# Three ways to feed float32 weights to TensorE in the mixer: split in two parts on ACT and VectorE, split by an accumulating DMA, or not split

## The chip, the cores and the metric

The kernel runs on one core of one Trainium2 chip. The metric is the time of one execution on the device in microseconds (us). One core has TensorE (PE, with its weight loads shown apart as PEld), VectorE (DVE), ScalarE (ACT), GpSimd (POOL) and SyncE (SP), which here issues loads, and 16 DMA engines that all transfers share.

## What is computed

Three layers in float32 on one sequence of 256 tokens with 1024 features. All of the change lies in the mixer of the first one.

```python
def mixer_sublayer(h, w_in, ...):               # h is 256 x 1024
    proj = h @ w_in
    conv_in, z, xbc, dt_raw, g_conv, g_ssm = jnp.split(proj, splits, axis=-1)
    a_half, b_half = jnp.split(conv_in, 2, axis=-1)
    u = a_half * sigmoid(b_half)
    u = causal_depthwise_conv(u, conv_dw_w, conv_dw_b)          # 31 taps
    y_conv = silu(layer_norm(u, ...)) @ w_conv_out
    xbc = silu(causal_depthwise_conv(xbc, ssm_conv_w, ssm_conv_b))
    xs, bm, cm = jnp.split(xbc, ...)
    dt = softplus(dt_raw + dt_bias)
    y = ssd_chunked_scan(xs, dt, -exp(a_log), bm, cm) + d_skip * xs   # 4 groups
    y = rmsnorm_per_group(y * silu(z)) * ssm_norm_w
    y_ssm = y @ w_ssm_out
    return (sigmoid(g_conv) * y_conv + sigmoid(g_ssm) * y_ssm) @ w_out
# block: h = rms_norm(x) * (1 + scale) + shift, where shift, scale = silu(c) @ w_ada + b
```

Behind it come a feed-forward layer, a gated-delta layer with an MLP and a gated-linear-attention layer with an MLP, each with a norm.

## The kernel before

**Items.** A weight matrix is cut into items of 128 x 1024 float32 (512 KB). One call of `w3` (L155) prepares one: SP loads it into a slot of the ring "raw", which has 6 (L150 to L153), and it is split into a rounded part hi and a remainder lo, both in TensorE's reduced float32 format (fp32r), in slots of the ring "w", which has 8, so four items. The slot of raw is free again when the splitting has read it. The activations h are split in the same manner into hh and hl, and `mm3` (L184 to L188) makes each product of three fp32r matmuls: hi by hi (L186), hi by lo (L187 or L188) and lo by hi.

**Two ways to split.** In the way called S here, ACT casts hi (L170) and DVE subtracts it from raw (L171). In the way called D, ACT writes minus raw to lo (L166), a DMA that POOL issues adds raw onto it while rounding (L167), and ACT casts hi (L168); so lo is the rounding remainder, and DVE has no part in it, but 512 KB more go through the DMA engines. A counter `nw` of the calls of `w3` decides: in the state space and the gates, calls after the 14th whose number isn't a multiple of 4 are D (L178), all others are S. By call numbers:
- 1 to 8, w_abe in `start`, S
- 9, w_dt (the step sizes dt), S
- 10 to 19, w_ab (gated input of the long convolution), 20 to 27, w_bc (B and C)
- 28 to 59, four groups g0 to g3, each with four items of w_xs and four of w_z
- 60 to 75, w_g (the gates).

So 34 of the state space's 51 items are D and 17 S; of the gates' 16, 12 are D and 4 S. Items of w_z make four products of 512 columns each (`proj_tok`, L204); all others make eight of 256 columns (`projA` with `mmA`).

**What runs beside it.** The 31 taps of the long convolution are 240 instructions on DVE (L501, from and to acc), spread over the time between w_ab and the merge, where `conv_ln` (L791) reads the result. The next layers' modulation weights (ada) are loaded into the same ring and reduced by DVE (L410). In each group, POOL and ACT build the right-hand sides srhs of the segment sums (L343, L349), PE multiplies (L352), ACT takes the exponential E (L679), DVE masks it (L681) and PE contracts it with xdt (L686). `mix_gates` (L718) leaves the tanh of the gates; `merge` then begins with w_ssm_out (psa<-yT).

**Order.** Each engine runs its own list of instructions in order. The lists are made ahead of time by a scheduler, from the program, its dependencies and the rings; SP's list of loads and POOL's list of accumulating DMAs are among them, so an instruction that waits holds up all behind it on its engine.

Of the kernel before, what the change touches and what calls it, by code (L numbers as in the profile page):

```python
# [18 lines left out]
P = 128  # L19
T = 256  # L20
D = 1024
# [45 lines left out]

NW = 14

# [41 lines left out]
class K:  # L111
    def __init__(self, ctx, tc, A):
        self.tc, self.nc, self.A = tc, tc.nc, A
        pool = lambda name, **kw: ctx.enter_context(tc.tile_pool(name=name, **kw))
        self.cp = pool("cp", bufs=1)
        self.px = pool("px", bufs=1)
        self.dp = pool("dp", bufs=1, space=bass.MemoryType.DRAM)
        self.wp = pool("wp", bufs=1)
        self.wx = self.big = self.sm = self.ps = self.kp = None
        self.n = self.nw = 0  # L120
        self.pending = None
        self.dma_lo = 0

# [31 lines left out]
    def w3(self, name, i, nk, extra=False):  # L155

        nc = self.nc
        if extra and self.wx is not None:
            hi, lo = (self.wx.tile([P, 1024], F32R, tag="wx", name=self.nm(v)) for v in ("xhi", "xlo"))
        else:  # L160
            hi, lo = (self.wp.tile([P, 1024], F32R, tag="w", bufs=8, name=self.nm(v)) for v in ("whi", "wlo"))
        t = self.raw(self.A[name][i])
        hi, lo = (v[:, : t.shape[-1]] for v in (hi, lo))
        self.nw += 1
        if self.dma_lo and self.nw > NW and self.nw % self.dma_lo:
            nc.scalar.activation(out=lo, in_=t, func=AF.Copy, scale=-1.0)  # L166
            nc.gpsimd.dma_start(out=lo, in_=t, accum_op=ALU.add)  # L167
            nc.scalar.copy(hi, t)  # L168
        else:
            nc.scalar.copy(hi, t)  # L170
            nc.vector.tensor_tensor(out=lo, in0=t, in1=hi.bitcast(F32), op=ALU.subtract)  # L171
# [18 lines left out]
    def mmA(self, out, w, x):  # L190


        for k in range(8):
            xh, xl = x(k) if callable(x) else (x[0][:, :, k, :], x[1][:, :, k, :])
            self.mm3(out, w[0][:, k], w[1][:, k], xh, xl, k == 0, k == 7)
# [9 lines left out]
    def proj_tok(self, name, i0, x, evac, early=False):  # L205
# [4 lines left out]
        def one(c, w, t):  # L210
            for k2 in range(2):
                k = 2 * c + k2
                self.mm3(b[t], x[0][:, t, k], x[1][:, t, k], w[0][:, k2], w[1][:, k2], k == 0, k == 7)

# [100 lines left out]

    def xpose_split(self, src, t, hi, lo, scale=None, bias=None, nk=8, ks=None, n=4):

        nc = self.nc
        n = min(nk, n)
        for k0 in ks or range(0, nk, n):  # L320
# [5 lines left out]
            if scale is None:  # L326
                nc.scalar.copy(h, b3)  # L327
                nc.vector.tensor_tensor(out=l, in0=b3, in1=h.bitcast(F32), op=ALU.subtract)  # L328
                continue
            f = self.smt([P, 4, P], "f")[:, :n]  # L330
            for kk in range(n):
# [185 lines left out]
    def start(self):  # L517
# [13 lines left out]
        for k in range(8):  # L531
            self.ada("w_ada_mix", k, mod)
            self.ada("w_ada_mix", 8 + k, mod)
            if k == 0:
                xn = [self.rms_tok(self.x[:, t]) for t in range(2)]
            self.ada_bias(mod, "b_ada_mix", k, k + 1)
            self.ada_bias(mod, "b_ada_mix", k + 8, k + 9)
            self.ada_scale(mod, "norm_mix_w", a, k, 1)
            for t in range(2):
                self.xpose_split(xn[t], t, h[0], h[1], a, mod[:, 0:8], ks=(k,), n=1)  # L540
            wh, wl = self.w3("w_abe", k, 6)
# [456 lines left out]
    def gdn(self, h):  # L998
# [44 lines left out]
        proj_z(0, True)  # L1043
        self.dma_lo = 5
        kT = self.bigt([P, 8, T], name="kT")
# [507 lines left out]
def tile_kernel(ctx, tc, A):  # L1553
    k = K(ctx, tc, A)
    nc = tc.nc
    with ExitStack() as st:
        k.kp = st.enter_context(tc.tile_pool(name="kp", bufs=1))
        with k.phase("mixer", 0, 0, 3, 3, 2):
            with k.phase("ssm", 1, 0, 0, 0, 0):
                k.dma_lo = 4  # L1560
                h, banks = k.start()
                yT, acc = k.state_space(h, banks)
                tg = k.mix_gates(h)
            k.dma_lo = 0
            with k.phase("mix", 0, 8, 0, 0, 0):
                mh = k.merge(yT, acc, tg)
    k.dma_lo = 0
    k.spill = k.dp.tile([P, 2, D], F32, name="spill")
    with k.phase("ffn", 0, 16, 2, 4, 2):
        h = k.feed_forward(mh)  # L1570
    with k.phase("gdn", 8, 0, 2, 3, 3):
        k.more_masks(M_R, M_LEV + 2)
        oT = k.gdn(h)
    k.dma_lo = 0
    with k.phase("mlp0", 0, 16, 2, 4, 2):
# [143 lines left out]
```

## Time and profile before

| | |
|---|---|
| runs of the kernel | 1437.17, 1437.42, 1441.13 us, median 1437.42 |
| the profiled execution's own time | 1445.81 us |
| its span (first to last instruction) | 1444.0 us |
| PE busy in the span | 1313.5 us (91%) |
| DVE, ACT, POOL busy | 994.4 (69%), 753.0 (52%), 160.7 us (11%) |
| loads by SP (hardware queue) | 224.08 MB, 45.0% of the DMA engines' time |
| DMAs by POOL (software queue) | 46.28 MB, 15.5% |

The span is read by stages, which the first matmuls of each kind mark on PE: `start` to 44.3 us, w_dt, w_ab, w_bc and g0's first w_xs items to 131, the groups' middles to 175, 214, 253, the end of g3 with the first gates to 283, the gates to 328.7, where `merge` begins. An engine's busy time against the length of a stage says how much of the stage it could explain; the waits say what ended the rest. PEclk is the granted TensorE clock as a share of the full 2.4 GHz.

### The profile page before, as it was taken

The numbers are of one execution on the slowest core, as the hardware profiler recorded it, in microseconds if no ns is written. First come the engines' busy times: TensorE is split into PE (matmuls) and PEld (weight loads), VectorE is DVE, ScalarE is ACT, GpSimd is POOL, SyncE is SP. The second block draws the span as 40 slices with busy tenths as digits, with TensorE's granted clock in tenths as the row PEclk, the third lists the DMA queues.
The fourth block names the chain that finished last, engine by engine and source line by source line (L and its number), as shares of the span: only waits on it lengthen the run. The fifth ranks groups of instructions, "written<-read, shape, count | busy, mean of one in ns | idle before, by whom it ended". The sixth has DMA issues, their size and how long they took to land. (4 is left out here: it accounts for less than half of the span.)

```text
span 1444.0 us, 21885 instructions
## 1 busy us (share of the span) xinstructions
PE 1313.5 (91%) x8408; PEld 1180.2 (82%) x8408; DVE 994.4 (69%) x1800; ACT 753.0 (52%) x1199; POOL 160.7 (11%) x176
## 2 busy tenths in 40 slices
PE   5899899879998999998768878899999998999997
PEld 4897788869987999977767766789997986788896
DVE  7878899669577665743679974865465796765453
ACT  4666687735446443636686523544353645454440
POOL 0212232210000000012511430000001000000000
PEclk9999999989899999999879989999999999999999
DMA  9899789998265765639458313765364313576430
GB/s 339 285 267 254 200 226 238 280 280 329 89 219 169 261 214 188 209 124 231 114 141 229 88 44 123 255 208 188 131 219 144 118 61 115 177 248 213 154 128 30
DMA packets 74616, 271.76 MB, mean 188 GB/s; under 512 B 8559, under 2 KB 8687, under 8 KB 74000
## 3 DMA queue, kind: packets, MB, share of 16 engines
q1 hardware_dynamic: 62208, 224.08, 45.0%
q0 software_dynamic: 12304, 46.28, 15.5%
q8 instruction: 66, 1.08, 0.3%
q14 instruction: 38, 0.31, 0.1%
HBM read 232.06 MB, written 2.10 MB: 162 GB/s over the span
## 5 line engine op out<-in xcount | busy, mean ns | idle before, releaser
L188 PE MATMUL psa<-hh,wlo 128*128 128x256 f32 x1448 | 419.3, 290 | 27.0 <-DMA wlo<-raw 24.9
L186 PE MATMUL psa<-hh,whi 128*128 128x256 f32 x1448 | 419.1, 290 | 2.3 <-ACT hh L180 1.3
L187 PE MATMUL psa<-hl,whi 128*128 128x256 f32 x1448 | 417.6, 288 | 0.8 <-DVE hl L181 0.5
L171 DVE TENSOR_TENSOR wlo<-raw,whi 128x1024 fp32r<-128x1024 f32 (+1 forms) x206 | 248.0, 1211 | 152.2 <-ACT whi L170 144.0
L170 ACT CAST whi<-raw 128x1024 fp32r<-128x1024 f32 (+1 forms) x206 | 213.4, 1041 | 216.4 <-PE psa L187 149.8
L188 PEld LDWEIGHTS psa<-hh,wlo 128*128 128x128 f32 x1448 | 284.1, 196 | 32.6 <-DMA wlo<-raw 28.5
L186 PEld LDWEIGHTS psa<-hh,whi 128*128 128x128 f32 x1448 | 284.4, 196 | 6.5 <-ACT hh L180 2.9
L187 PEld LDWEIGHTS psa<-hl,whi 128*128 128x128 f32 x1448 | 283.7, 196 | 3.9 <-DVE hl L181 1.8
L171 DVE TENSOR_TENSOR xlo<-raw,xhi 128x1024 fp32r<-128x1024 f32 x100 | 121.1, 1221 | 64.5 <-ACT xhi L170 64.1
L170 ACT CAST xhi<-raw 128x1024 fp32r<-128x1024 f32 x100 | 104.8, 1050 | 95.7 <-DMA raw<-in_w_mlp 60.7
L186 PE MATMUL psb<-xhi,hid 128*128 128x512 f32 x344 | 136.2, 396 | 1.0 <-ACT hid L327 0.9
L188 PE MATMUL psb<-xhi,hidl 128*128 128x512 f32 x344 | 136.2, 396 | 0.0
L187 PE MATMUL psb<-xlo,hid 128*128 128x512 f32 x344 | 135.7, 395 | 0.0
L501 DVE SCALAR_TENSOR_TENSOR acc<-u,vecs,acc 128x229 f32<-128x229 f32 (+28 forms) x240 | 104.8, 479 | 0.3
L166 ACT ACTIVATE wlo<-raw 128x1024 fp32r<-128x1024 f32 x69 | 73.0, 1058 | 49.0 <-PE psa L187 25.5
L187 PE MATMUL psa<-wlo,hh 128*128 128x512 f32 x208 | 83.4, 402 | 5.4 <-DVE wlo L171 3.6
L167 POOL DMA_DIRECT2D wlo<-raw x69 | 60.1, 870 | 247.4 <-ACT wlo L166 200.8
L186 PE MATMUL psa<-whi,hh 128*128 128x512 f32 x208 | 84.1, 406 | 2.1 <-ACT hh L180 1.5
L410 DVE CUSTOM_DVE_ANT_0 raw<-raw,g 128x1024 f32<-128x1024 f32 x48 | 58.6, 1220 | 37.6 <-DMA raw<-in_w_ada_ffn 21.9
L188 PE MATMUL psa<-whi,hl 128*128 128x512 f32 x208 | 82.9, 401 | 0.6 <-DVE hl L181 0.6
L188 PEld LDWEIGHTS psb<-xhi,hidl 128*128 128x128 f32 x344 | 64.7, 188 | 15.3 <-DVE hidl L181 0.3
L186 PEld LDWEIGHTS psb<-xhi,hid 128*128 128x128 f32 x344 | 64.8, 188 | 15.0 <-ACT hid L327 1.4
(388 smaller groups left out, 2230.8 us busy)
## 6 DMA issues: line engine op xcount, KB each, us to landing
raw<-in_w_mlp SPq DMA_DIRECT2D x120, 512.0 KB, 4.1
wlo<-raw POOLq DMA_DIRECT2D x69, 512.0 KB, 7.2
raw<-in_w_ffn_in SPq DMA_DIRECT2D x40, 512.0 KB, 4.2
raw<-in_w_ada_mix SPq DMA_DIRECT2D x24, 512.0 KB, 5.8
raw<-in_w_ada_ffn SPq DMA_DIRECT2D x24, 512.0 KB, 4.5
raw<-in_w_qkv SPq DMA_DIRECT2D x24, 512.0 KB, 5.6
raw<-in_w_ffn_down SPq DMA_DIRECT2D x22, 512.0 KB, 4.2
raw<-in_w_xs SPq DMA_DIRECT2D x16, 512.0 KB, 5.2
```

The lines of the kernel that those rows point to most:

```text
L166: nc.scalar.activation(out=lo, in_=t, func=AF.Copy, scale=-1.0)
L167: nc.gpsimd.dma_start(out=lo, in_=t, accum_op=ALU.add)
L170: nc.scalar.copy(hi, t)
L171: nc.vector.tensor_tensor(out=lo, in0=t, in1=hi.bitcast(F32), op=ALU.subtract)
L186: mm(out, ah, bh, start=start, stop=False)
L187: mm(out, ah, bl, start=False, stop=False)
L188: mm(out, al, bh, start=False, stop=stop)
L410: self.nc.vector.tensor_tensor_reduce(out=w, in0=w, in1=self.sc, scale=1.0, scalar=0.0, op0=ALU.mult, op1=ALU.add, accum_out=mod[:, i : i ...
L501: nc.vector.scalar_tensor_tensor(out=o, in0=i, scalar=taps[:, j : j + 1], in1=o, op0=ALU.mult, op1=ALU.add)
```

## The change

Three forms of an item are named by letters, and a string gives the turn: the form of call number `nw` is `form[nw % len(form)]`. N is new: the raw item itself is the operand of float32 matmuls, one for each product in place of three, with h kept in float32 beside its two halves. Nothing is split for it, and its slot of raw stays taken until PE has read it.

```diff
-NW = 14
+FORM_SSM = "NDNS"
+FORM_GATES = "SD"
+FORM_GDN = "SDDDD"
...
+        self.nw += 1
+        form = self.form[self.nw % len(self.form)]
+        if form == "N":
+            return (self.raw(self.A[name][i]).rearrange("p (k c) -> p k c", k=nk),)
...
-        self.nw += 1
-        if self.dma_lo and self.nw > NW and self.nw % self.dma_lo:
+        if form == "D":
...
         for k in range(8):
+            if len(w) == 1:
+                self.nc.tensor.matmul(out, w[0][:, k], x[2][:, :, k, :], start=k == 0, stop=k == 7)
+                continue
...
+                if len(w) == 1:
+                    self.nc.tensor.matmul(b[t], x[2][:, t, k], w[0][:, k2], start=k == 0, stop=k == 7)
+                else:
+                    self.mm3(b[t], x[0][:, t, k], x[1][:, t, k], w[0][:, k2], w[1][:, k2], k == 0, k == 7)
...
-            f = self.smt([P, 4, P], "f")[:, :n]
+            f = self.smt([P, 4, P], "f")[:, :n] if full is None else full[:, t, k0 : k0 + n]
...
+                h = (*h, self.xt().rearrange("p t (k c) -> p t k c", k=8))
...
-                k.dma_lo = 4
                 h, banks = k.start()
+                k.form = FORM_SSM
                 yT, acc = k.state_space(h, banks)
+                k.form = FORM_GATES
                 tg = k.mix_gates(h)
-            k.dma_lo = 0
+            k.form = "S"
```

The 51 items of the state space become 25 N (the even numbers), 13 D and 13 S; w_dt, number 9, becomes D. Of the N items 17 are of the kind with eight products of 256 columns (5 of w_ab, 4 of w_bc, 8 of w_xs) and 8 of w_z with four products of 512. The gates become 8 S and 8 D in turn. In the gated-delta layer the string gives the same forms as before. The float32 h takes the buffer that held the input x, which has been read by then; the second half of the gates takes it over later. The instructions of PE from the start of `merge` on, and those of all later layers, are the same in both kernels. In the rows below the numbers behind names tell tiles apart.

On PE, at the start of the state space (hh, hl are the halves of h, x the float32 h, whi, wlo the halves of an item, pss the bank of w_dt, psa that of w_ab). Before:

```order
L188 MATMUL psb_109<-hh_102,wlo_467 128x256
L186 MATMUL pss_618<-hh_102,whi_619 128x256
L187 MATMUL pss_618<-hl_103,whi_619 128x256
L188 MATMUL pss_618<-hh_102,wlo_620 128x256
L186 MATMUL pss_618<-hh_102,whi_619 128x256
L187 MATMUL pss_618<-hl_103,whi_619 128x256
```

Now:

```order
L194 MATMUL psb_109<-hh_102,wlo_452 128x256
L201 MATMUL psa_670<-x_136,raw_671 128x256 x2
L192 MATMUL pss_603<-hh_102,whi_604 128x256
L193 MATMUL pss_603<-hl_103,whi_604 128x256
L201 MATMUL psa_670<-x_136,raw_671 128x256 x5
L194 MATMUL pss_603<-hh_102,wlo_605 128x256
```

The products of w_dt now stand behind seven of the eight float32 products of item 10, and wait at L194 for a lo that comes by DMA.

On POOL, from the first group to the second (wlo is lo of an item, srhs the right-hand side of a segment sum, yrs a group's norm). Before:

```order
L167 DMA wlo_1901<-raw_1902 128x1024
L167 DMA wlo_1952<-raw_1953 128x1024
L167 DMA wlo_1983<-raw_1984 128x1024
L343 TENSOR_TENSOR srhs_1770<-mk,dah 128x512
L343 TENSOR_TENSOR srhs_1795<-mk,dah 128x512
L343 TENSOR_TENSOR srhs_1812<-mk,dah 128x512
L343 TENSOR_TENSOR srhs_2132<-mk,dah 128x512
L167 DMA wlo_2057<-raw_2058 128x1024
```

Now:

```order
L173 DMA wlo_1613<-raw_1614 128x1024
L173 DMA wlo_1735<-raw_1736 128x1024
L355 TENSOR_TENSOR srhs_1502<-mk,dah 128x512
L355 TENSOR_TENSOR srhs_1527<-mk,dah 128x512
L355 TENSOR_TENSOR srhs_1544<-mk,dah 128x512
L355 TENSOR_TENSOR srhs_1796<-mk,dah 128x512
L308 TENSOR_TENSOR yrs_1568<-rsq_1569,mhalf 128x2
```

Fewer accumulating DMAs lie between, but the second segment sum of the first group still stands behind those of the second group's items (wlo_1735 is of its second w_z item).

On ACT, in the middle of the gates (tg and x take the tanh of a finished bank). Before:

```order
L166 ACTIVATE wlo_3316<-raw_3317 128x1024
L728 ACTIVATE tg_3004<-psa_3145 128x512
L168 CAST whi_3315<-raw_3317 128x1024
L166 ACTIVATE wlo_3355<-raw_3356 128x1024
L168 CAST whi_3354<-raw_3356 128x1024
L166 ACTIVATE wlo_3386<-raw_3387 128x1024
L728 ACTIVATE tg_3004<-psa_3214 128x512
L168 CAST whi_3385<-raw_3387 128x1024
L170 CAST whi_3424<-raw_3426 128x1024
```

Now:

```order
L172 ACTIVATE wlo_2773<-raw_2774 128x1024
L174 CAST whi_2772<-raw_2774 128x1024
L176 CAST whi_2811<-raw_2813 128x1024
L172 ACTIVATE wlo_2842<-raw_2843 128x1024
L741 ACTIVATE tg_2532<-psa_2672 128x512
L174 CAST whi_2841<-raw_2843 128x1024
L176 CAST whi_2880<-raw_2882 128x1024
```

Three items by DMA and one by DVE have become one and one.

## Rows read from the trace of the kernel before

**Rows 1.** Busy time by stage: the length of the stretch, then busy time and (instructions) of PE, PEld, DVE, ACT, POOL, the granted clock, the mean busy share of the 16 DMA engines, and GB/s.

```profile
44.30:131.00 86.70, 78.50 (x602) 76.67 (x603) 73.76 (x178) 59.12 (x89) 16.35 (x22) 0.96 0.95 261
131.00:175.00 44.00, 39.75 (x234) 34.68 (x233) 35.49 (x74) 30.14 (x58) 10.38 (x12) 0.92 0.81 215
175.00:214.00 39.00, 37.42 (x239) 32.76 (x238) 36.82 (x79) 32.48 (x61) 10.50 (x12) 1.00 0.88 223
214.00:253.00 39.00, 36.58 (x233) 31.92 (x232) 35.75 (x72) 30.33 (x58) 11.60 (x13) 1.00 0.90 235
253.00:283.00 30.00, 26.04 (x200) 23.98 (x199) 21.36 (x38) 22.34 (x44) 8.80 (x8) 1.00 0.98 283
283.00:328.70 45.70, 34.75 (x252) 33.59 (x251) 28.36 (x59) 16.73 (x20) 5.15 (x6) 0.89 1.00 290
328.70:364.90 36.20, 34.88 (x291) 34.68 (x290) 34.40 (x51) 18.74 (x19) 0.00 (x0) 1.00 0.85 308
```

**Rows 2.** Waits of PE in the state space, 44.3 to 283 us: us in total, times, longest.

```profile
PE psb L686 <- DVE E L681: 5.4, 5, 3.9
PE psa L188 <- DMA wlo<-raw: 3.0, 1, 3.0
...
PE psa L187 <- DMA wlo<-raw: 1.0, 1, 1.0
...
PE pss L352 <- POOL srhs L343: 0.8, 2, 0.5
```

**Rows 3.** Waits of PE in the gates, 283 to 328.7 us.

```profile
PE psa L188 <- DMA wlo<-raw: 9.0, 3, 5.0
PE psa L188 <- DVE wlo L171: 1.9, 2, 1.3
```

**Rows 4.** Waits of SP's queue of loads, 44.3 to 283 us.

```profile
SPq L152 <- DMA wlo<-raw: 154.2, 38, 8.0
```

**Rows 5.** The DMA queues in 44.3 to 253 us (packets, MB, share of the 16 engines' time), and the accumulating DMAs and the loads of w_xs issued in it (how many, KB each, us from issue to landing).

```profile
q0 software_dynamic: 5028, 18.35, 47.3%
q1 hardware_dynamic: 8636, 31.42, 41.9%
...
wlo<-raw POOLq DMA_DIRECT2D x36, 512.0 KB, 7.1
raw<-in_w_xs SPq DMA_DIRECT2D x16, 512.0 KB, 5.2
```

**Rows 6.** The same in 253 to 329 us.

```profile
q1 hardware_dynamic: 4382, 15.99, 59.3%
q0 software_dynamic: 1596, 5.77, 39.4%
...
wlo<-raw POOLq DMA_DIRECT2D x10, 512.0 KB, 9.8
```

**Rows 7.** PE's timeline where fp32r and float32 matmuls meet at 256 columns: start, us, line, and records (x16 are eight calls of L791, two records each).

```profile
363.80 0.28 PE L187 MATMUL psa<-yT,xhi 128*128 128x256 f32 x1
...
365.00 0.28 PE L188 MATMUL psa<-yT,xlo 128*128 128x256 f32 x1
365.12 3.61 PE L791 MATMUL pss<-acc,ones 128*128 128x256 f32 x16
368.39 0.47 PE L186 MATMUL psa<-yT,whi 128*128 128x256 f32 x1
```

**Rows 8.** PE's timeline at 512 columns, fp32r: the first matmuls of two products of w_z that follow each other.

```profile
180.32 0.39 PE L186 MATMUL psa<-whi,hh 128*128 128x512 f32 x1
...
181.00 0.39 PE L186 MATMUL psa<-whi,hh 128*128 128x512 f32 x1
```

**Rows 9.** The same at 512 columns in float32: the row ahead and one call of L694 (two records).

```profile
142.74 0.83 PE L670 MATMUL psb<-c,xsT 128*128 128x128 f32 x6
143.41 1.02 PE L694 MATMUL psb<-g 128*128 128x512 f32 x2
```

**Rows 10.** Groups of instructions in 44.3 to 283 us: count, busy us and mean ns of one, then idle time before them and its releasers.

```profile
L501 DVE SCALAR_TENSOR_TENSOR acc<-u,vecs,acc 128x232 f32<-128x232 f32 (+28 forms) x182 | 79.7, 483 | 0.0
...
L166 ACT ACTIVATE wlo<-raw 128x1024 fp32r<-128x1024 f32 x40 | 42.4, 1059 | 24.1 <-PE psa L187 17.5 <-issue 4.7 <-ACT whi L168 0.9
L167 POOL DMA_DIRECT2D wlo<-raw x40 | 34.9, 873 | 150.4 <-ACT wlo L166 113.9 <-ACT th L583 26.8 <-ACT g L621 6.4
...
L171 DVE TENSOR_TENSOR wlo<-raw,whi 128x1024 fp32r<-128x1024 f32 x19 | 23.1, 1218 | 0.6 <-ACT whi L170 0.5
```

**Rows 11.** The start of the state space: POOL's last row before its first accumulating DMA.

```profile
43.31 2.44 POOL L405 TENSOR_SCALAR vecs<-vecs 128x8 f32<-128x8 f32 x6
```

**Rows 12.** The same stretch on DVE: the subtraction for w_dt.

```profile
48.05 1.22 DVE L171 TENSOR_TENSOR wlo<-raw,whi 128x1024 fp32r<-128x1024 f32 x1 [0.51 <-ACT whi L170]
```

**Rows 13.** DVE's timeline in g0, ahead of the E (L681, 148.35 us) that PE waits for (in brackets the idle time before and what ended it).

```profile
140.24 1.23 DVE L410 CUSTOM_DVE_ANT_0 raw<-raw,g 128x1024 f32<-128x1024 f32 x1 [3.27 <-DMA raw<-in_w_ada_ffn]
```

**Rows 14.** The stretches behind PE's longer waits, in the columns of the first group.

```profile
148.20:155.00 6.80, 5.92 (x25) 5.63 (x25) 5.24 (x11) 3.30 (x11) 1.04 (x1) 0.52 0.93 281
301.80:305.20 3.40, 2.74 (x13) 2.74 (x14) 0.71 (x2) 0.37 (x1) 0.00 (x0) 0.53 1.03 389
318.80:325.70 6.90, 4.32 (x20) 4.33 (x21) 3.49 (x8) 1.05 (x1) 0.00 (x0) 0.52 1.04 307
```

**Rows 15.** Groups of instructions of PE in the gates, 283 to 328.7 us.

```profile
L188 PE MATMUL psa<-hh,wlo 128*128 128x256 f32 x84 | 26.2, 312 | 10.9 <-DMA wlo<-raw 9.0 <-DVE wlo L171 1.9
```

More of the change, by code (lines that the diff above doesn't have):

```diff
@@ L121, in __init__ @@
         self.pending = None
-        self.dma_lo = 0
+        self.form = "S"
     def phase(self, name, big, wx, a, b, s):
@@ L212, in one @@
                 k = 2 * c + k2
-                self.mm3(b[t], x[0][:, t, k], x[1][:, t, k], w[0][:, k2], w[1][:, k2], k == 0, k == 7)
+                if len(w) == 1:
+                    self.nc.tensor.matmul(b[t], x[2][:, t, k], w[0][:, k2], start=k == 0, stop=k == 7)
+                else:
+                    self.mm3(b[t], x[0][:, t, k], x[1][:, t, k], w[0][:, k2], w[1][:, k2], k == 0, k == 7)
         if early:
@@ L314, in softplus, with xpose_split @@
         nc.vector.scalar_tensor_tensor(out=out, in0=x, scalar=0.0, in1=p, op0=ALU.max, op1=ALU.add)
-    def xpose_split(self, src, t, hi, lo, scale=None, bias=None, nk=8, ks=None, n=4):
+    def xpose_split(self, src, t, hi, lo, scale=None, bias=None, nk=8, ks=None, n=4, full=None):
         nc = self.nc
@@ L539, in start @@
             for t in range(2):
-                self.xpose_split(xn[t], t, h[0], h[1], a, mod[:, 0:8], ks=(k,), n=1)
+                self.xpose_split(xn[t], t, h[0], h[1], a, mod[:, 0:8], ks=(k,), n=1, full=h[2])
             wh, wl = self.w3("w_abe", k, 6)
@@ L1043, in gdn @@
         proj_z(0, True)
-        self.dma_lo = 5
+        self.form = FORM_GDN
         kT = self.bigt([P, 8, T], name="kT")
@@ L1559, in tile_kernel @@
             with k.phase("ssm", 1, 0, 0, 0, 0):
-                k.dma_lo = 4
                 h, banks = k.start()
+                k.form = FORM_SSM
                 yT, acc = k.state_space(h, banks)
+                k.form = FORM_GATES
                 tg = k.mix_gates(h)
-            k.dma_lo = 0
+            k.form = "S"
             with k.phase("mix", 0, 8, 0, 0, 0):
                 mh = k.merge(yT, acc, tg)
-    k.dma_lo = 0
     k.spill = k.dp.tile([P, 2, D], F32, name="spill")
@@ L1573, in tile_kernel @@
         oT = k.gdn(h)
-    k.dma_lo = 0
+    k.form = "S"
     with k.phase("mlp0", 0, 16, 2, 4, 2):
```

## The prediction

> **What bounds the kernel now.** I read the span by stages first [rows 1]. In the state space (44.3 to 283 us) PE is busy for 218.3 of 238.7 us, DVE for 203.2, ACT for 174.4: PE is the bound, with 20.4 us of gaps, and in the stage to 131 us the DMA engines are at 0.95 as well. The gates are another matter: PE has 34.75 busy us in 45.7, DVE and ACT less, the DMA engines 1.00. In the first 36 us of the merge PE (34.88) and DVE (34.40) are both full.
>
> Then the waits. In the state space the longest are for E (5.4 us, once 3.9) and for a lo that comes by DMA (3.0 and 1.0) [rows 2]. In the gates three waits for such a lo make 9.0 us, against 1.9 for a lo of DVE's [rows 3]. Behind the long waits the granted clock is about half (0.52 and 0.53, which is the level of 1.2 GHz) for 6.8, 3.4 and 6.9 us [rows 14]. Last the transfers: between 253 and 329 us the two queues together fill 98.7% of the DMA engines' time, 39.4 of it with 11 accumulating DMAs' worth of bytes [rows 6]. SP's loads wait for accumulating DMAs 38 times, 154 us in all [rows 4], since a slot of raw comes free only when they have read it. So two resources count: PE in the state space, the DMA engines in the gates.
>
> **The change, part by part.** I make the sum against the profiled execution (1445.81 us, span 1444.0) and carry the difference to the median of the runs, 1437.42, which is 8.4 us lower; stages that the change does not touch cancel.
>
> *Float32 products on PE.* An fp32r matmul of 256 columns starts 0.12 us after the one before (ten steps from 363.80 to 365.00), so a split product takes 0.36. The eight float32 calls of L791 end 3.45 us after the fp32r matmul ahead of them (365.28 to 368.73): 0.431 each [rows 7]. An N item of eight products costs 0.57 us more; 17 of them 9.7. At 512 columns a split product takes 0.68 (180.32 to 181.00) [rows 8], and a float32 call 0.86 (from the end of the row ahead, 143.57, to 144.43) [rows 9]: 4 x 0.18 = 0.72 more for an item, 5.8 for eight. Together **+15.5 us**, on the engine that bounds the stage, so I let none of it hide. Below that it can come only by gaps that close, which are counted next.
>
> On the price of float32 the Trainium skill ("FP8 and Floating Point Precision", section "TensorE Precision Notes") says that a true FP32 matmul makes four passes through the array. Row and rule differ: four steps of 0.12 would be 0.48 where the row has 0.431; by the rule the term would be about 24 us, and I go by the row.
>
> *w_dt by DMA.* POOL is at its scalars until 45.75 us [rows 11]; then come ACT's 1.06 (mean of L166), POOL's 0.87 (L167) [rows 10] and a landing of 7.1 [rows 5], so lo is there at about 55, where DVE's was at 49.3 [rows 12]. PE has seven float32 products (3.0 us) and two thirds of the first split product to do meanwhile, and reaches that point at about 49 to 50; six us of wait would follow if nothing moved, none if POOL is earlier or the landing is as quick as the queue is empty here. I take **+2** (0 to +5).
>
> *What leaves the state space.* 21 accumulating DMAs: at 47.3% of 208.7 us for 36 of them, one takes 2.74 us of all the engines [rows 5], 58 us in all, and with it half the reason that loads come late. ACT loses 46 casts net of about 1.05 us [rows 10] (21 D items fewer, two casts each, and 4 S items fewer), some 48 of its 174 us. DVE loses 4 subtractions of 1.22. From that I take the two waits for a lo (4.0); of the E wait 3.3, because ahead of that E in DVE's order stands an ada reduction that waited 3.27 for its load [rows 13]; and of the half clock behind it 3 (5.92 busy us at 0.52 would be about 3) [rows 14]. **-10**, with 0 and -14 as ends: 0 if other waits close in, -14 if half of the remaining 10 us of gaps goes too. The long convolution's 240 taps on DVE (182 in this stage, 79.7 us [rows 10]) stay covered by PE's products as before; without that cover a tap is 0.44 us (79.7 by 182).
>
> *The gates.* 12 D become 8. Four DMAs less are 11 us of the engines' time in a stretch that has no spare DMA time [rows 6]. The floor is 84 products of 0.36, 30.2 us, in a stage of 45.7 [rows 1, 15]: 15.5 us could go, made of 10.9 of waits [rows 15] and 4.6 of half clock. I take 11 of transfer time and 2 of the clock, **-13**, ends -5 (the S items' latency takes half the waits' place) and -15.5. The four subtractions more on DVE (4.9 us) lie beside 17 idle us there.
>
> *The merge.* Before, DVE works on taps there while the splits wait; after, the order has the taps done at its start. PE's gap there is 1.3 us [rows 1]: **-1**, ends 0 and -1.3. From the merge on PE's order is the same, so a gain stays.
>
> Sum: 15.5 + 2 - 10 - 13 - 1 = **-6.5 us**, 1439.3 in the profiled execution's measure, about **1431** against the median; I say 1430.
>
> **The rivals.** *The gates wait for turns of the ring, not for bandwidth.* Then fewer DMAs help only where their own landing was the last thing: a D item still needs load, cast, POOL and a landing of 9.8 us [rows 6], and every second item is one. The gates give 5 to 6, the state space its 10 against 17.5: the sum is between 0 and -3, **1436**. For it speaks that the waits in the gates are three of at most 5.0 us and not many short ones [rows 3]; against it that the engines show no idle share. The Trainium skill ("Perfetto Trace Analysis", section "Roofline") bounds a single core by its 16 DMA engines at about 435 GB/s; this stage has 290 [rows 1] with the engines at 1.00, so by that figure there would be bandwidth left and this rival would hold, while the busy share says that a DMA which reads, adds and rounds takes more of the engines than its bytes. Chance 0.20.
>
> *POOL's order holds up the segment sums: slower.* An N item holds its slot of raw until PE is done with it, so the load of an item two or three behind starts later. In each group the second srhs stands behind the accumulating DMAs of the next group's items on POOL. If such a load starts only after the last product of the slot's holder, its landing (5.2 [rows 5]), the cast (1.06) and POOL's 0.87 [rows 10] make 7.1 us before that srhs can begin, and PE may have no more than one w_z item in between (4 x 0.86): 3.7 us of wait for a group, 15 for four. Before, such waits were 0.8 in all [rows 2], but then a slot came free without PE. It decides from the point where more than 3.4 us of the 7.1 lie behind the holder's last product. With all of it the sum is +8: **1445**. Chance 0.18.
>
> *All gaps close.* State space -14 and gates -15.5, no wait for w_dt: the sum is -15 to -17, **1421**. ACT's and the DMA engines' relief speaks for it; DVE, still at 85% of the stage, against. Chance 0.10.
>
> *Float32 items cost four steps*, with 256 columns 0.48 and with 512 0.91: +24 in place of +15.5, the sum +2, **1439**. The two rows of this trace speak against it; they are of other operands than weights just loaded, but at the same shapes. Chance 0.04.
>
> **How the numbers follow.** The forecast has 0.48, with 1424 to 1436 as its own range. A measurement of this kernel can tell about 0.3% from no change, 4.3 us, so faster is below 1433.1 and slower above 1441.7. Faster: 0.43 of the forecast's 0.48, the third rival's 0.10 and a little of the first: 0.54. Same: 0.05, most of the first rival and the fourth: 0.27. Slower: the second rival and a tail: 0.19. For the range I take from 1420, below the third rival's value, to 1446, above the second's; beyond either end remain mishaps of more than one kind at once.
>
> **What would show it.** In the profile after, records of an N item 0.43 us (w_z: 0.86) apart per product show the first term. The first psa<-yT on PE at about 322 to 323 us in place of 328.7 shows the sum; the first matmul of the gates later than before by about 7 would show PE's price, and the gates shorter by 13 their part. The DMA share in the gates should fall below 0.95, and PE's waits for a lo by DMA there below 3 us; if the share falls and the waits stay, the first rival is right. Waits of L352 for srhs by POOL of more than 5 us are the second. A wait at the first L194 into pss shows w_dt's price. I am wrong above all if ACT's and the DMA engines' relief closes none of PE's gaps in the state space: then the sum is +3.5 with the gates as forecast, and slower with any miss there.

## The result: slower by 0.66%, outside the range

The changed kernel took 1449.58 us in the median of five runs (1443.98 to 1450.29), the kernel before 1438.48 (1437.17 to 1441.13): a ratio of 1.0066, 95% interval 1.0044 to 1.0088. That is 9.5 us slower by the ratio (11.1 by the medians), where 6.5 to 7.5 us faster was forecast.

The stages after, in the columns of [rows 1] (length, busy time and instructions of PE, PEld, DVE, ACT, POOL, granted clock, DMA share, GB/s); the merge begins on PE at 332.6 us, where the first profile of before had 328.7:

```profile
44.30:131.00 86.70, 75.21 (x458) 68.39 (x459) 70.72 (x178) 37.07 (x63) 8.94 (x14) 0.96 0.72 218
131.00:175.00 44.00, 40.89 (x220) 32.24 (x220) 38.45 (x87) 23.52 (x52) 9.44 (x8) 1.00 0.50 141
175.00:214.00 39.00, 36.10 (x194) 27.48 (x192) 35.29 (x75) 21.83 (x49) 6.77 (x7) 1.00 0.51 148
214.00:253.00 39.00, 36.47 (x197) 27.89 (x195) 35.51 (x74) 20.20 (x46) 7.21 (x6) 1.00 0.51 152
253.00:283.00 30.00, 28.31 (x158) 21.58 (x157) 28.81 (x57) 17.75 (x36) 5.30 (x5) 1.00 0.85 258
283.00:332.50 49.50, 46.06 (x366) 45.25 (x366) 32.46 (x57) 24.67 (x36) 6.04 (x7) 0.97 0.92 275
332.50:368.70 36.20, 34.85 (x291) 34.65 (x290) 25.11 (x27) 18.72 (x19) 0.00 (x0) 1.00 0.91 340
```

The rows show what was freed and what it bought. They are cut at the same times as those of before, so the changed kernel, which is behind, has slightly earlier work in each. In the groups (131 to 253 us) the DMA engines' share fell from 0.81 to 0.90 before to a half, ACT's busy time in a stage from 30 to 32 us to 20 to 24. PE, in the same stretches, is as busy as before (113.5 us for 113.8): its gaps did not close. The merge's first 36 us are as long as they were, although DVE now has 25.11 busy us in place of 34.40. The gates have waits of PE left that are small:

```profile
PE psa L194 <- DVE wlo L177: 1.8, 1, 1.8
PE psa L194 <- DMA wlo<-raw: 1.0, 1, 1.0
```

against 9.0 and 1.9 in [rows 3]. In the state space the waits have changed names, not size (44.3 to 283 us; compare [rows 2]):

```profile
PE pss L630 <- DVE bc L526: 4.7, 1, 4.7
PE pss L364 <- POOL srhs L355: 3.9, 5, 2.1
PE pss L649 <- DVE xsT L526: 2.9, 3, 1.2
PE pss L584 <- issue: 2.2, 1, 2.2
PE psb L699 <- DVE E L694: 2.2, 4, 1.1
```

E gives 2.2 in place of 5.4, lo by DMA has left the list's head; the wait for bc was 2.6 in the first profile of before and is 4.7, srhs was 0.8 and is 3.9. Ahead of the wait for bc (117.6 to 122.3 us) DVE has no idle time from 110 us on; its list there holds taps of the short and of the long convolution in turn.

The start of the state space, PE's timeline (start, us, line, records, in brackets the idle time before):

```profile
46.98 1.03 PE L201 MATMUL psa<-x,raw 128*128 128x256 f32 x4
49.67 0.39 PE L192 MATMUL pss<-hh,whi 128*128 128x256 f32 x1 [1.67 <-ACT whi L174]
49.90 0.28 PE L193 MATMUL pss<-hl,whi 128*128 128x256 f32 x1
50.02 2.32 PE L201 MATMUL psa<-x,raw 128*128 128x256 f32 x10
53.36 0.39 PE L194 MATMUL pss<-hh,wlo 128*128 128x256 f32 x1 [1.02 <-DMA wlo<-raw]
```

Two things are read here. Five float32 products end 2.16 us after the fp32r matmul ahead of them (50.18 to 52.34), 0.43 each, as priced from L791 [rows 7]. And w_dt is held up twice, by ACT's cast (which in the way D comes after the one of minus raw) and by the DMA; it is done at 56.3 us, and what hangs on it comes later still. The first sums of dt (L584) start at 71.2 us after a gap of 2.2, where in the kernel before they started at 66.8 without one, and the first segment sum waits 2.1 us for srhs until 156.6.

The first profile of before was a long one (1445.81 us). A second one of the same kernel, of the run a_before_again below, took 1437.33 us (span 1435.5), close to the median of the runs; it is the better partner for the changed kernel's profile, whose execution took 1449.87. Its stages, cut at its own start of the merge and at the first product with conv_ln's result:

```profile
44.30:283.00 238.70, 219.63 (x1525) 201.73 (x1526) 203.89 (x442) 176.56 (x312) 57.00 (x66) 0.98 0.92 249
283.00:322.60 39.60, 31.50 (x228) 30.31 (x227) 24.26 (x50) 14.43 (x17) 5.04 (x6) 0.91 1.00 297
322.60:383.20 60.60, 58.63 (x439) 57.80 (x438) 47.93 (x78) 27.87 (x35) 1.28 (x2) 0.92 0.63 231
```

and PE's waits in its gates, 283 to 322.6 us:

```profile
PE psa L188 <- DMA wlo<-raw: 5.0, 3, 3.1
PE psa L188 <- DVE wlo L171: 3.1, 2, 1.8
```

So the merge begins at 323 us in an ordinary run of before, 10 us ahead of the changed kernel's 333, about the difference of the times; and the 9.0 us of waits on which the gates' term rested are 5.0 in this run.

These rows hold the whole account up to the merge. From 44.3 us on PE is busy for 251.1 us and idle for 27.2 in the second profile of before, busy for 263.0 and idle for 25.2 in the changed kernel: 11.9 us more of work and only 2.0 us less of gaps, with work at the lower clock counted as long as it took. (Against the first profile, with 31.4 idle us, it is 10.0 more and 6.2 less.) The merge itself, up to the first product with conv_ln's result, is as long as in the second profile of before (60.6):

```profile
332.40:392.50 60.10, 58.68 (x438) 57.86 (x437) 36.59 (x48) 28.16 (x36) 1.28 (x2) 0.91 0.63 232
```

The signs of the gates that the prediction named did appear: their DMA share in the rows above is 0.92, and the waits for a lo by DMA are 1.0. From the first of the gates' 128 products to the merge it is 59.8 us, where the second profile of before has 72.9 (a part of that is order: 17 matmuls of g3 that stood behind this point now stand ahead of it). But the first of these products comes at 272.8 us in place of 250.0 (253.3 in the first profile), 20 to 23 later where about 7 was named.

### The profile page after: what moved, and what is told of

It is laid out like the page before. It is cut to its first block, busy times and chain, and to the rows that moved or that the text cites. A ratio compares the mean times of both kernels' runs of the same rounds, so it can differ in the third digit from the quotient of the medians.

```text
span 1447.4 us, 21402 instructions
## 1 busy us (share of the span) xinstructions
PE 1323.4 (91%) x8240; PEld 1168.5 (81%) x8240; DVE 994.6 (69%) x1800; ACT 706.5 (49%) x1149; POOL 141.7 (10%) x151
## 5 line engine op out<-in xcount | busy, mean ns | idle before, releaser
L194 PE MATMUL psa<-hh,wlo 128*128 128x256 f32 x1312 | 376.7, 287 | 14.9 <-DMA wlo<-raw 13.0
L192 PE MATMUL psa<-hh,whi 128*128 128x256 f32 x1312 | 380.0, 290 | 1.9 <-ACT hh L186 1.2
L193 PE MATMUL psa<-hl,whi 128*128 128x256 f32 x1312 | 375.8, 286 | 0.9 <-DVE hl L187 0.9
L194 PEld LDWEIGHTS psa<-hh,wlo 128*128 128x128 f32 x1312 | 254.6, 194 | 19.1 <-DMA wlo<-raw 16.1
L192 PEld LDWEIGHTS psa<-hh,whi 128*128 128x128 f32 x1312 | 255.2, 194 | 5.9 <-ACT hh L186 2.9
L193 PEld LDWEIGHTS psa<-hl,whi 128*128 128x128 f32 x1312 | 254.5, 194 | 4.2 <-DVE hl L187 2.0
L194 PE MATMUL psb<-xhi,hidl 128*128 128x512 f32 x344 | 136.2, 396 | 0.0
L513 DVE SCALAR_TENSOR_TENSOR acc<-u,vecs,acc 128x244 f32<-128x244 f32 (+25 forms) x240 | 107.6, 489 | 1.4 <-ACT acc L506 1.0
L194 PEld LDWEIGHTS psb<-xhi,hidl 128*128 128x128 f32 x344 | 64.7, 188 | 15.5 <-DVE hidl L187 0.4
L193 PE MATMUL psa<-wlo,hh 128*128 128x512 f32 x176 | 71.4, 408 | 6.1 <-DVE wlo L177 3.6
L193 PEld LDWEIGHTS psb<-xlo,hid 128*128 128x128 f32 x344 | 64.6, 188 | 13.6
L172 ACT ACTIVATE wlo<-raw 128x1024 fp32r<-128x1024 f32 x44 | 46.6, 1058 | 52.8 <-PE psa L193 19.7
L422 DVE CUSTOM_DVE_ANT_0 raw<-raw,g 128x1024 f32<-128x1024 f32 x48 | 58.9, 1227 | 19.4 <-DMA raw<-in_w_ada_mix 11.3
L194 PE MATMUL psa<-whi,hl 128*128 128x512 f32 x176 | 71.3, 408 | 0.6 <-DVE hl L187 0.6
```

The lines of the kernel that those rows point to most:

```text
L192: mm(out, ah, bh, start=start, stop=False)
L193: mm(out, ah, bl, start=False, stop=False)
L194: mm(out, al, bh, start=False, stop=stop)
L422: self.nc.vector.tensor_tensor_reduce(out=w, in0=w, in1=self.sc, scale=1.0, scalar=0.0, op0=ALU.mult, op1=ALU.add, accum_out=mod[:, i : i ...
L513: nc.vector.scalar_tensor_tensor(out=o, in0=i, scalar=taps[:, j : j + 1], in1=o, op0=ALU.mult, op1=ALU.add)
```

## The experiments

Fifteen kernels ran, each beside the kernel before on the same chip. All ratios are to that kernel, with their 95% intervals; one per cent is 14.4 us. "E" is where PE first contracts with E (the first group), "merge" where its first product of w_ssm_out starts, both in us in the one profile of each run. That one profile is not always a typical run: a_dt_split's, b_before_dt_dma's and d_h_kept's are the quickest of their runs, d_no_price's the slowest of its six.

| run | median us | ratio | interval | E | merge |
|---|---|---|---|---|---|
| before, second profile (a_before_again) | 1437.61 | 1.0003 | 0.9977 to 1.0028 | 148 | 323 |
| the changed kernel | 1449.58 | 1.0066 | 1.0044 to 1.0088 | 159 | 333 |
| a_gates_only | 1436.44 | 0.9976 | 0.9954 to 0.9999 | 148 | 318 |
| a_ssm_only | 1452.75 | 1.0100 | 1.0071 to 1.0129 | 159 | 343 |
| a_dt_split | 1444.54 | 1.0042 | 1.0016 to 1.0067 | 152 | 328 |
| b_dose0 | 1460.77 | 1.0137 | 1.0104 to 1.0169 | 167 | 354 |
| b_dose13 | 1432.08 | 0.9947 | 0.9930 to 0.9964 | 153 | 325 |
| b_dose38 | 1442.30 | 1.0021 | 1.0005 to 1.0037 | 147 | 325 |
| b_before_dt_dma | 1449.87 | 1.0070 | 1.0051 to 1.0089 | 154 | 339 |
| c_d0_early_S | 1446.27 | 1.0047 | 1.0025 to 1.0069 | 154 | 335 |
| c_d0_phase | 1444.91 | 1.0047 | 1.0023 to 1.0071 | 159 | 330 |
| c_after_early_S | 1437.87 | 0.9993 | 0.9970 to 1.0016 | 152 | 329 |
| c_d13_early_S | 1433.11 | 0.9958 | 0.9936 to 0.9979 | 149 | 320 |
| d_no_price | 1429.37 | 0.9923 | 0.9899 to 0.9947 | 146 | 314 |
| d_split_unused | 1485.21 | 1.0317 | 1.0283 to 1.0351 | 181 | 375 |
| d_h_kept | 1436.71 | 0.9976 | 0.9955 to 0.9997 | 147 | 315 |

**a_before_again**, the kernel before, unchanged.

> The kernel before once more, unchanged, for a second profile: its first profile took 1445.8 us, 7 us more than the median of its runs. Theory: the profile fell on a run with more time at half clock, and a second one has a higher mean clock than 0.963 and a span of about 1437. Rival: the profiler costs it 7 us each time, then the span is again about 1444 at 0.963.

The span was 1435.5 us and the clock 0.967: the first profile had fallen on a long run.

**a_gates_only**, on the kernel before:

```diff
                 yT, acc = k.state_space(h, banks)
+                k.dma_lo = 2
                 tg = k.mix_gates(h)
```

> The kernel before, with the gates alone in the new turn (S, D), so 8 accumulating DMAs there in place of 12. Theory 1 (the gates' gain is their own and the state space pays TensorE's price for N): the gates shrink by about 10 us, as between the two traces, and the time is about 1429 against 1438.5. Rival (the gates got faster only because the state space left loads and slots behind): the gates stay within 3 us of before, time about 1437.

The gain is 0.24%, 3.5 us, where theory 1 expected 10; by the time the rival's 1437 came closer. The gates did become shorter, by 5.3 us from their first product to the merge, which is neither theory 1's 10 nor within the rival's 3. PE's waits in the gates (283 to 317.5 us) and then in the merge (317.5 to 380.9):

```profile
PE psa L188 <- DVE wlo L171: 4.6, 4, 2.3
```

```profile
PE psa L188 <- DVE wlo L171: 2.2, 2, 1.5
PE pss L791 <- DVE acc L501: 1.9, 1, 1.9
```

No wait for a DMA is left, and those for DVE's subtraction have grown from 3.1 to 4.6; the merge then waits 1.9 us for the last taps, a wait that the second profile of before does not have. In the stretch ahead of the merge the DMA engines stay full:

```profile
283.00:317.50 34.50, 29.88 (x243) 29.07 (x242) 24.86 (x49) 14.18 (x17) 3.44 (x4) 1.00 1.00 302
317.50:380.90 63.40, 59.28 (x439) 57.91 (x439) 52.66 (x88) 28.14 (x35) 1.28 (x2) 0.92 0.63 228
```

So a share of 1.00 is no sign that PE waits for bandwidth: here PE waits for no DMA beside it. Over all of the gates, from their first product to the merge, the second profile of before and this run have:

```profile
249.90:322.80 72.90, 60.46 (x449) 57.20 (x448) 47.27 (x93) 38.77 (x63) 12.97 (x14) 0.95 1.00 293
250.10:317.70 67.60, 59.15 (x449) 56.12 (x449) 47.15 (x86) 35.51 (x59) 10.34 (x11) 0.95 0.93 278
```

Some 10 us of the engines' time went (1.00 of 72.9 to 0.93 of 67.6), as four DMAs of 2.74 would have it, and 5.3 us of the stage. The merge gave 2.8 of these back: 63.4 us for 60.6.

**a_ssm_only**, on the changed kernel:

```diff
-FORM_GATES = "SD"
+FORM_GATES = "SDDD"
```

> The changed kernel, with the gates in the old turn (S, D, D, D). Theory 1: all of the price of N without the gates' gain: 10 us above the changed kernel, about 1459. Rival: the gates are quick here too, and the time is that of the changed kernel within 3 us, about 1450.

1.0100: against the changed kernel's 1.0066 the gates are worth 4.9 us here (3.2 by the medians; the intervals overlap). By the time that is nearer to the rival, yet the stage itself did as theory 1 has it. The two kernels have the same order of PE up to the gates; from the gates' first product to the merge, a_ssm_only and then the changed kernel:

```profile
271.90:343.10 71.20, 57.52 (x430) 55.67 (x430) 39.60 (x71) 35.57 (x58) 10.73 (x12) 0.90 0.93 272
272.80:332.60 59.80, 54.70 (x430) 53.17 (x429) 42.33 (x73) 30.91 (x52) 8.52 (x9) 0.97 0.90 268
```

and PE's largest wait there in a_ssm_only, where the changed kernel has 1.0:

```profile
PE psa L194 <- DMA wlo<-raw: 9.7, 3, 5.9
```

So the new turn makes the gates 11.4 us shorter here, not far from the forecast 13. But a_ssm_only's merge then takes 54.6 us where the changed kernel's takes 60.1 (the rows stand above and in the last section): 5.5 of the gain are gone again at the lower clock, in these two profiles. The two single edits, +14.4 and -3.5 us, add up to 10.9 where the whole change has 9.5. By the time, the state space holds the whole loss.

**a_dt_split**, on the changed kernel:

```diff
-        form = self.form[self.nw % len(self.form)]
+        form = "S" if self.nw == 9 else self.form[self.nw % len(self.form)]
```

> The changed kernel, with item 9 (w_dt) split on ACT and VectorE as before, all else the same. Theory 1 (the loss is TensorE's price for 25 N items, some 14 us): it gains 1 to 3 us at most, about 1447. Rival (the loss is the start of the state space, where the wait for w_dt's lo delays dt and all that hangs on it): it gains 5 us or more, 1444 or less, and the gap before the first sum of dt at 70.9 us goes.

1444.54, 5.0 us less by medians (by the ratios 3.5, 1.0066 to 1.0042, with intervals that overlap). The first contraction with E comes 7 us earlier and the merge 5. This lies between the theories: w_dt's way is a third to a half of the loss, and the gap at the sums of dt is gone (they start at 63.4 us).

**b_dose0, b_dose13, b_dose38**, on a_dt_split; the turn NDNS becomes

```diff
-FORM_SSM = "NDNS"
+FORM_SSM = "DDDS"   # b_dose0;  b_dose13: "NDDS";  b_dose38: "NNNS"
```

> The changed kernel with item 9 (w_dt) split on ACT and VectorE and no N item: the state space's turn is D, D, D, S; float32 h is still kept, the gates are S, D. Theory 1 (each N item costs TensorE 0.57 to 0.72 us that nothing hides): against the 25 N items of the run before (1444.5) 15.5 us of products fall away and a few us of waits come back; about 1433, and the merge begins on TensorE at about 317 us, as with the new gates alone. Rival (the state space is bound by splitting and transfers, and N pays for itself): 1443 or more.

> As b_dose0, with 13 N items (turn N, D, D, S; w_xs, w_z, w_ab and w_bc each have some). Theory 1: half way between none and 25, about 1439, the merge at about 322 us. Rival (a few N items where the splits are late pay for themselves, and only many cost): as quick as b_dose0 or quicker, 1433 or less.

> As b_dose0, with 38 N items and 13 S, no accumulating DMA in the state space (turn N, N, N, S). Theory 1: 13 items more than the 25 cost TensorE 8 us more, and the transfers that go bring nothing: about 1452, the merge at about 335 us. Rival (accumulating DMAs on POOL's queue are what holds the segment sums up, so without any the waits go): not above the 25 N items' 1444.5.

The turns give 12 and 37 N items, one less than the names and the expectations say. Theory 1's slope fell, at both ends. Without any N item the kernel is the slowest of the four, by 16 us (1.0137); with 12 it is the fastest (0.9947, faster than both kernels of this case), with 25 it has 1.0042, with 37 1.0021. What an N item saves is thus not a constant. PE's waits in b_dose0 (44.3 to 283 us):

```profile
PE pss L649 <- DVE xsT L526: 12.6, 3, 5.8
PE psa L194 <- DMA wlo<-raw: 8.2, 7, 2.4
PE psa L192 <- DVE c L513: 7.9, 2, 5.5
```

Two of the three are DVE's work for the short convolution. Ahead of that work DVE itself stands idle, at an ada reduction (L422) whose load has not landed, and behind it PE waits:

```profile
119.17 1.23 DVE L422 CUSTOM_DVE_ANT_0 raw<-raw,g 128x1024 f32<-128x1024 f32 x1 [11.29 <-DMA raw<-in_w_ada_ffn]
122.48 0.55 PE L192 MATMUL psa<-hh,whi 128*128 128x256 f32 x1 [5.51 <-DVE c L513]
152.05 1.23 DVE L422 CUSTOM_DVE_ANT_0 raw<-raw,g 128x1024 f32<-128x1024 f32 x1 [7.06 <-DMA raw<-in_w_ada_ffn]
157.09 0.45 PE L649 MATMUL pss<-ident,xsT 128*128 128x128 f32 x1 [5.76 <-DVE xsT L526]
```

Five such pairs (PE at 122.5, 157.1, 197.9, 242.7 and 270.6 us) make 20.5 us of PE's waits; the profile names the load in three of them and no releaser of DVE in the others. The reduction is work for a later layer; it only stands ahead in DVE's list. In the changed kernel no reduction waits over 1.5 us between 44.3 and 283 us. Why the loads come late in this turn is not shown.

**b_before_dt_dma**, on the kernel before:

```diff
-        if self.dma_lo and self.nw > NW and self.nw % self.dma_lo:
+        if self.dma_lo and (self.nw > NW or self.nw == 9) and self.nw % self.dma_lo:
```

> The kernel before, with item 9 (w_dt) split by accumulating DMA, all else the same. Theory 2 (w_dt by DMA delays dt, and the segment sums and all of the first group behind it, by about 5 us): about 1443, the first contraction with E on TensorE 4 us or more later than at 147.4 to 148.8 us. Rival (what w_dt lost in the changed kernel comes of its place between N items, not of its way): within 2 us of before.

1.0070: that one item by DMA costs the kernel before 10 us, as much as the whole change and twice what theory 2 expected. E is 6.6 us later (154.2 for 147.6). That the old rule kept this item from the DMA was worth that.

**c_d0_early_S and c_d0_phase**, on b_dose0:

```diff
# c_d0_early_S
-        form = "S" if self.nw == 9 else self.form[self.nw % len(self.form)]
+        form = "S" if self.nw <= 14 else self.form[self.nw % len(self.form)]
# c_d0_phase
-FORM_SSM = "DDDS"
+FORM_SSM = "SDDD"
```

> b_dose0 (no N item, turn D, D, D, S) with items 9 to 14 all split on ACT and VectorE, as the kernel before has them. Theory 3 (what made b_dose0 slow, 1460.8, are its accumulating DMAs among the first items, whose loss the later groups pass on): about 1438, the first contraction with E at about 148 us in place of 166. Rival (it is the place of the S items in a group, at the last item of w_xs and of w_z in place of the first): stays above 1450.

> b_dose0 with the turn moved by one (S, D, D, D: S at the first item of w_xs and of w_z, as before), early items 10, 11, 13 and 14 by DMA. Theory 3 (the early DMAs are the loss): as slow as b_dose0, above 1452. Rival (the place in the group): about 1440, and the waits for xsT of 5 to 6 us are gone.

Theory 3 and its rival are each half right: each edit takes b_dose0 from 1.0137 to 1.0047, 13 us, and both together (d_h_kept) give 0.9976. The early accumulating DMAs and the place of the S item in a group each cost 10 to 13 us. Each edit leaves DVE one wait of over 5 us at an ada reduction in the state space, 8.7 and 10.2 us, where b_dose0 has three, of 11.3, 7.1 and 7.0.

**c_after_early_S and c_d13_early_S**: the same line as c_d0_early_S, on a_dt_split and on b_dose13.

> The changed kernel with items 9 to 14 split on ACT and VectorE: 22 N items are left in place of 25, 12 D. Theory 3: with the early items as before only the price of 22 N (13.5 us) against the 22 D or S that it saves is left; if the saving of splits is worth nothing in the groups, about 1446, as without this edit but with w_dt split (1444.5); if the early items were all of the loss, 1436 or less.

> b_dose13 (turn N, D, D, S; 1432.1, the best so far) with items 9 to 14 split on ACT and VectorE, so 11 N. Theory 3: the early DMAs (10, 13, 14) cost here too, so it gains 3 us or more, about 1428. Rival (N item 12 among them had already given back what the early DMAs cost): within 2 us of 1432.

The changed kernel with the first six items as before (22 N and 11 D left, not 12) comes to 0.9993, no difference from the kernel before; 10.5 us of loss are gone by one condition. Its single profile has the merge where a_dt_split's has it (329 and 328 us), but that one was the quickest of a_dt_split's runs, so how much items 10 to 14 add to w_dt's part is not settled by the traces. With 12 N items the same edit changes nothing (0.9958 and 0.9947): the rival was right there.

**d_no_price**, on a_dt_split, leaves out products of the N items, and so part of what is computed (one of eight, in w_z one of four):

```diff
             if len(w) == 1:
+                if k == 4:
+                    continue
...
                 if len(w) == 1:
+                    if t == 1 and k2 == 1:
+                        continue
```

> a_dt_split (the changed kernel with w_dt split on ACT and VectorE, 1444.5) with part of the products of its N items left out: one of eight at 256 columns, one of four at 512, so that an N item takes TensorE about what a split one took (3.0 for 2.9 us, 2.6 for 2.7); 17 x 0.43 + 8 x 0.86 = 14.2 us of products go. Theory 1 (TensorE bounds the state space, so the price of float32 passes whole to the time): about 1431, the merge begins 13 to 14 us earlier than at 327.6. Rival (the state space is bound by VectorE and by the turns of the ring, and the price lies beside that): 1439 or more, the merge no more than 6 us earlier.

1429.37 and 0.9923: 15.2 us less by medians (17 by the ratios) for 14.2 us of products, and the merge 13.8 us earlier (313.98 for 327.80). Theory 1 holds for the price: within the intervals, some 5 us, it passes whole.

**d_split_unused**, on a_dt_split:

```diff
         if form == "N":
-            return (self.raw(self.A[name][i]).rearrange("p (k c) -> p k c", k=nk),)
+            t = self.raw(self.A[name][i])
+            hi, lo = (self.wp.tile([P, 1024], F32R, tag="w", bufs=8, name=self.nm(v)) for v in ("whi", "wlo"))
+            nc.scalar.activation(out=lo, in_=t, func=AF.Copy, scale=-1.0)
+            nc.gpsimd.dma_start(out=lo, in_=t, accum_op=ALU.add)
+            nc.scalar.copy(hi, t)
+            return (t.rearrange("p (k c) -> p k c", k=nk),)
```

> a_dt_split with the 25 N items also split by accumulating DMA, into tiles that nothing reads: TensorE's products are the same, but no cast and no transfer is saved. Theory 4 (saving the splits of 25 items is worth about 5 us, which is why the price of 15.5 showed as 10.5): about 1450, the merge at 332 to 334 us. Rival A (the saving is worth far more, as b_dose0's 1460.8 says): 1460 or more. Rival B (it is worth nothing): within 2 us of 1444.5.

Theory 4 missed by 35 us: 1485.21, as rival A has it. Its waits (44.3 to 283 us) are of all kinds:

```profile
PE pss L654 <- DVE xsT L531: 7.6, 4, 3.7
PE psb L704 <- DVE E L699: 6.9, 6, 4.5
PE pss L635 <- DVE bc L531: 6.8, 2, 6.0
PE psa L206 <- issue: 5.5, 1, 5.5
PE psa L206 <- ACT whi L168: 5.2, 1, 5.2
PE psa L199 <- DMA wlo<-raw: 4.1, 1, 4.1
```

The run is an upper bound, not a measure: the unused halves also take slots of the ring "w", and a slot of raw is now held for both the DMA and PE. It does say that 25 unused splits by DMA, put on top of 12 D and 14 S, cost 41 us in this order. It does not say how much of that is the splits and how much the slots.

**d_h_kept**, on a_dt_split:

```diff
-        form = "S" if self.nw == 9 else self.form[self.nw % len(self.form)]
+        form = "S" if self.nw <= 14 else self.form[self.nw % len(self.form)]
-FORM_SSM = "NDNS"
+FORM_SSM = "SDDD"
```

> a_gates_only (1436.4) with float32 h kept, in the changed kernel's code: items 9 to 14 S, then S, D, D, D, no N item. Theory (keeping h in the buffer that held x costs nothing, and b_dose0's slowness is of its turn and its early items alone): within 3 us of 1436.4, the merge at about 318 to 322 us. Rival (the kept h itself, by the order that it brings, costs what the runs without N items lost): 1442 or more.

0.9976, the same as a_gates_only: keeping h costs nothing.

## Why the prediction was wrong

The terms, against what the runs give (one per cent as 14.4 us):

| term | forecast | measured | from |
|---|---|---|---|
| float32 products on PE | +15.5 | +15 to +17, for the 14.2 us of them left out | d_no_price against a_dt_split |
| w_dt by DMA | +2 (0 to +5) | +3.5 to +5 | the changed kernel against a_dt_split |
| what leaves the state space | -10 (0 to -14) | -7.6 by the time, -1.1 at the merge in one profile of each | d_no_price (0.9923) against d_h_kept (0.9976) |
| the gates, with the merge | -14 (-5 to -16.8) | -3.5 to -4.9 | a_gates_only; a_ssm_only against the changed kernel |

The measured ones are uncertain by 3 to 5 us each, from their intervals. They add up to about +8.5, where the whole change has 9.5.

**The step that failed is the return on what was taken off the other engines: "-10" in the state space and, most of all by the time, "I take 11 of transfer time and 2 of the clock, -13" in the gates.** In terms of PE, the sum took 7 us of waits from the state space and 11 from the gates and gave 2 to w_dt: some 16 us of gaps less. Up to the merge they became 2.0 us less against an ordinary run (27.2 to 25.2), 6.2 against the long one, while the work grew by 10 to 12. In 44.3 to 283 us the gaps went from 19.1 (20.4 in the first profile) to 21.7, in the rest from 8.1 to 3.4. So the sign under "I am wrong above all", that none of PE's gaps in the state space close, is the one that came.

*The gates* are worth 3.5 to 4.9 us by the time, 8 to 10 less than the term, more than half of the miss of some 16. Three things made the difference. The 9.0 us of waits were those of one long run; an ordinary one has 5.0 (a_before_again). In the kernel before some 10 us of transfer time went and the stage became only 5.3 us shorter, since the waits passed to DVE's subtractions and the last taps (4.6, 2.2 and 1.9 us in a_gates_only), which I had named only as the lower end. And where the stage did become 11.4 us shorter, in the changed kernel against a_ssm_only, "so a gain stays" failed: the merge, the same order of PE, took 5.5 us more at the lower clock. The first rival had the mechanism of the second of these. It took its relief in the state space for granted, and its terms were added wrongly: they give about +1, not 0 to -3. (Of the other sums, the lower end of the relief, -10 and half of 10 more, is -15 and not -14.)

**The sum of the state space was +7.5 and came to +14.4 (a_ssm_only), or +12.9 (the changed kernel against a_gates_only).** Its largest part, the price, was right, and the reason too: PE bounds the stage, and d_no_price shows the price coming off whole. w_dt was mis-sized, by 1.5 to 3 us: I counted the wait at its product and not what hangs on dt, which is why E came 12 us later in the changed kernel and only 5 later with w_dt split (159.4 and 152.2 for 147.6); b_before_dt_dma shows 10 us for the same edit alone, beyond the bound of 5. The relief has -7.6 by the time, with intervals as wide as some 5 us, and the two traces bear out no more than 1.1 at the merge. One part of it came as forecast: no ada reduction waits long for its load there any more, and the waits for E fell from 5.4 to 2.2. Others took their place, for bc, behind a DVE that was busy throughout with taps, and for srhs. So in this place the taps did not "stay covered by PE's products". And the number is of one mix: b_dose0, d_split_unused and the phase run show that what a saved split is worth changes with the place of the item. The reason that I gave ("half the reason that loads come late") I can't show: in the trace after, the DMA share in the groups fell by some 40% and ACT's time by almost a third, and the waits were for DVE (bc, xsT) and for srhs. The parts that I left at bounds of both signs were the ones that decided.

**The second rival, POOL's order, is not the cause of the slower time.** Waits for srhs rose from 0.8 to 3.9 us, not to 15, and 2.1 of them are the one of the first group, which a_dt_split (1.5 in all in its waits) loses along with w_dt's delay. The fourth (four steps in a float32 product) is refuted by 0.43 in the trace after. The Trainium skill ("FP8 and Floating Point Precision", "TensorE Precision Notes") speaks of four passes and gives no time for one; the 24 us took a pass to be an fp32r step of 0.12 us, and it is this estimate that the trace does not bear out, not the page.

**What stays open.** Why the turn of D and S alone is worth 10 to 20 us between kernels with nearly equal counts. In b_dose0 the late ada loads ahead of DVE's work are the visible part; but DVE's and POOL's lists come out in another order for each turn, and the runs do not separate the order from the lateness of the loads and splits. Whether the merge gives a gain back in general is open too: it did in two pairs of single profiles. And how much of the last 5 us between a_dt_split and c_after_early_S is real: the medians say 6.7, one profile of each (a_dt_split's being its quickest run) says no difference at the merge.

The best version that computes all is b_dose13: turn N, D, D, S, w_dt split on ACT and VectorE, gates S, D: 0.9947 (0.9930 to 0.9964), 7.6 us faster than the kernel before.

## What to carry to other kernels

A saved resource was worth no more here than what the bounding engine waited for it, in a run that is typical: look at two profiles before a wait of one of them becomes a term, and don't read a transfer share of 1.00 as a queue that the bounding engine stands in. Work added to the bounding engine was paid in full; work taken from the others was paid back only down to the next wait. So forecast the gaps of the bounding engine as a whole, and ask which engine will end each of them next. The first items of a stage are not like the rest: what later work hangs on (here dt) should go the quickest way, whatever the turn says. And in an engine's list, look for work of another stage that waits for a load: all that stands behind it waits too.

## What the runs showed of the hardware

The same merge, the same instructions of PE in the same order, takes from 55 to 63 us up to the first product with conv_ln's result, as the granted clock falls. In a_ssm_only it is 54.6 us:

```profile
343.00:397.60 54.60, 54.01 (x437) 53.19 (x437) 35.44 (x47) 26.31 (x34) 1.28 (x2) 1.00 0.65 242
```

at a granted clock of 1.00, in a_gates_only 63.4 at 0.92 (the row above; 1.9 of it is the wait for the taps), in the second profile of before 60.6 at 0.92. So a gain ahead of this stage can be given back in it by the clock alone. Runs of one kernel lay up to 20 us apart (1432.06 to 1452.03 for 29 runs of the kernel before), and its two profiles have the merge 6 us apart (328.7 and 322.6), so no single profile here settles less than that.
